# Moving columns read in two alternating halves, and activations placed two lines from the weights, in a four-layer hybrid backbone

## The chip, the cores and the metric

The kernel runs on one core of one Trainium2 chip. The metric is the device time of one execution in microseconds; of several runs the median counts.

## What is computed

The reference runs DEPTH = 2 layers over 256 latent tokens and 256 context tokens of width 1024. Each layer has a token mixer (a gated linear recurrence, RG-LRU, and a chunked gated attention, HGRN2, both in both directions, fed by one input projection) and a feed-forward part with a depthwise convolution. Nearly all arithmetic is dense products of tokens with weights:

```python
zc = hc @ lp['w_in']                 # 1024 x 9216, per layer
zl = hl @ lp['w_in']
...
p_rg = y_rg @ lp['w_proj_rg']        # 1024 x 1024
p_hg = y_hg @ lp['w_proj_hg']        # 1024 x 1024
m = jax.nn.sigmoid(z[..., O_GA:O_GA + D_MODEL]) * p_rg + jax.nn.sigmoid(z[..., O_GB:O_GB + D_MODEL]) * p_hg
return m @ lp['w_out']               # 1024 x 1024
...
u = h @ w_up                         # 1024 x 5632
return (jax.nn.silu(g) * v) @ w_down # 2816 x 1024
```

The second layer computes the outputs of the latent tokens alone, so its later products are 256 tokens wide and those of the first layer 512.

## The kernel before

Every large product is made of three TensorE products in float32r, a 4-byte format of fewer bits: an operand x is split into hi = round(x) and lo = x - hi, and hi·hi + hi·lo + lo·hi is accumulated in PSUM. Weights arrive by DMA in tiles `raw` of 1 MB; `piece` (L221) splits half a tile into `whi` (ScalarE, L233) and `wlo` (VectorE, L234). Activations lie split as well: `hi`, `lo` (the normalised input), `yh`, `yl`, `xg`, `xs`, `fh`, `fl`, `mh`, `ml`.

A matmul here has a stationary operand of 128 x 128, loaded by a weight load (LDWEIGHTS) of its own ahead of each matmul, and a moving operand of 128 x 512 or 128 x 256 columns whose product is written to as many columns of PSUM. There are two places that issue the large ones:

- `mm3` (L237, matmuls on L239 to L241) issues the three products of one k-slice of 128 rows. `feat_group` (L250) calls it for the products with features on the partitions: the weights are stationary and the activations move, 512 or 256 columns. `values` (L698) calls it with the tokens stationary and 256 columns of weights moving, and `recur` (L578) for the recurrence's gates of the first layer, with the weights `gwh`, `gwl` stationary and `xs` moving.
- `tok_product` (L490, matmuls on L500, L501, L503) is used for w_out and the down projection: the activations are stationary and 512 columns of weights move.

The trace writes a matmul as output<-stationary and moving by name, in alphabetical order, so `mm<-hi,whi` with 512 or 256 columns has `whi` stationary, and `mm<-whi,hi` is that of `values`, with `hi` stationary.

Smaller products (the attention's, the transposes, the gates of the second layer) are in plain float32, are issued elsewhere and read their columns in one run; TensorE makes two passes over a plain float32 product, and the trace has a record for each.

The order of the work is that of the Python code, with a list `side` of small steps (the modulation vectors, largely `ada_sums` on VectorE, L302) mixed in by `aside`, and a scheduler that moves instructions by priority. Where a tile lies in a partition of SBUF follows from the order of the pools and the sizes of the tiles in them. `home` (L69) takes the first piece of three pools for a filler tile; FILL gives its columns of 4 bytes. All tiles of the large products have sizes that are multiples of 256 bytes, so the fillers set where each begins within 256 bytes. With FILL = (24, 16, 24) the moving operand of every large product and the stationary operand that is loaded during it both begin 128 bytes past a multiple of 256.

Of the kernel before, what the change touches and what calls it, by code (L numbers as in the profile page):

```python
# [8 lines left out]
F32 = mybir.dt.float32  # L9
# [5 lines left out]
P = 128  # L15
# [23 lines left out]
PRI = 300  # L39
FINE = 6  # L40

FILL = (24, 16, 24)


def sub(t, off, dims):
    b = t[:]
    return bass.AP(tensor=b.tensor, offset=b.offset + off, ap=[list(b.ap[0])] + [list(d) for d in dims])


class Net:  # L50
# [18 lines left out]
    def home(self, ctx):  # L69
        for pool, n in zip((self.const, self.sm, ctx.enter_context(self.tc.tile_pool(name="pad", bufs=1, side="right"))),  # L70
                           FILL):
            if n:
# [10 lines left out]
    def psum(self):  # L83
        return self.mm.tile([P, 512], F32, tag="mm", name=self.nm("mm"))
# [5 lines left out]
    def act(self, **kw):  # L90
        ins = self.nc.scalar.activation(**kw)  # L91
        if self.last is not None:
            self.tc.add_manual_dep(ins.ins if hasattr(ins, "ins") else ins, self.last, mybir.DependencyInfo(
                mybir.DependencyClass.NoSync, mybir.DependencyReason.DATA), reason="table order")
        self.last = (ins.ins if hasattr(ins, "ins") else ins).name
        return ins
# [139 lines left out]

    def mm3(self, out, L, R, start, stop):  # L237
        nc = self.nc
        nc.tensor.matmul(out=out, lhsT=L[0], rhs=R[0], start=start, stop=False)  # L239
        nc.tensor.matmul(out=out, lhsT=L[0], rhs=R[1], start=False, stop=False)  # L240
        nc.tensor.matmul(out=out, lhsT=L[1], rhs=R[0], start=False, stop=stop)  # L241
# [64 lines left out]
    def ada_cols(self, l, m_shift, m_scale, g, store, key, ns=0):  # L306
# [22 lines left out]
        def three(i, m, j, row):  # L329
            ps = self.aux()  # L330
            nc.tensor.transpose(ps[:, 0:64 * n], row, self.ident[0:64 * n, 0:64 * n])
            close(i, m, j, sub(ps, 0, [[32, 2], [64, n]]))
# [157 lines left out]
    def tok_product(self, w, nk, act, psum):  # L490
        nc = self.nc
        pss = [[psum() for _ in range(2)] for _ in range(2)]
        pcs = {}

        def step(i, k):
            hi, lo = pcs[k]
            ah, al = act(k, i)
            for n in range(2):
                out = pss[i][n]
                nc.tensor.matmul(out=out, lhsT=ah, rhs=hi[:, n, :], start=k == 0, stop=False)  # L500
                nc.tensor.matmul(out=out, lhsT=ah, rhs=lo[:, n, :], start=False, stop=False)  # L501
            for n in range(2):
                nc.tensor.matmul(out=pss[i][n], lhsT=al, rhs=hi[:, n, :], start=False, stop=k == nk - 1)  # L503

        for k0 in range(0, nk, 2):
            raw = self.raw()
            r3 = raw.rearrange("p (k n) -> p k n", k=2)
            nc.sync.dma_start(out=r3, in_=w[k0 * P:(k0 + 2) * P, :].rearrange("(k p) n -> p k n", p=P))
            for kk in range(2):
                pcs[k0 + kk] = self.piece(r3[:, kk, :].rearrange("p (a b) -> p a b", a=2), (2, 512))  # L510
            ks = [k for k in (k0, k0 + 1) if k < nk - 3]
            for i in range(2):
                for k in ks:
                    step(i, k)
        for i in range(2):
            for k in range(nk - 3, nk):
                step(i, k)
        return pss


    def rg_phase(self, l, h, need_ctx, dr, first, more):
        nc, tc, I = self.nc, self.tc, self.ins
# [8 lines left out]
        with tc.tile_pool(name=self.nm("rg"), bufs=1, reuse_waits="tile") as pool:  # L531
# [2 lines left out]
            t2 = lambda tag, n: lambda: pool.tile([P, 2, 512], F32, tag=tag, name=self.nm(tag), bufs=n)  # L534
            R, Q, A = t2("r", 2), t2("q", 2), t2("a", 2)
            xc, g_t, gw = {}, {}, {}

            def conv(m, ps):
                t = m
                acc = XG()  # L540
                cw = lambda j: C["rcw"][:, j * 8 + t:j * 8 + t + 1]
                nc.scalar.activation(out=acc, in_=ps, func=AF.Identity, scale=cw(1), bias=C["rcb"][:, t:t + 1])
                a3, p3 = acc.rearrange("p (s t) -> p s t", s=2), ps.rearrange("p (s t) -> p s t", s=2)
                for j, (o, i) in ((0, (slice(1, S), slice(0, S - 1))), (2, (slice(0, S - 1), slice(1, S))),
                                  (3, (slice(0, S - 2), slice(2, S)))):
                    nc.vector.scalar_tensor_tensor(out=a3[:, :, o], in0=p3[:, :, i], scalar=cw(j), in1=a3[:, :, o],
                                                   op0=ALU.mult, op1=ALU.add)
                xc[t] = acc
# [13 lines left out]
            def gate_w(t):  # L562
                raw = pool.tile([P, 4, P], F32, tag="gwr", name=self.nm("gwr"), bufs=2)
                nc.gpsimd.memset(raw, 0.0)
                for u in range(2):
                    for gi, nme in enumerate(("rg_wa", "rg_wx")):
                        nc.sync.dma_start(out=raw[u * 64:(u + 1) * 64, gi::2, u * 64:(u + 1) * 64],
                                          in_=I[nme][l, :, 2 * t + u].rearrange("d i j -> i d j"))
                if exact:
                    gw[t] = (raw, raw)  # L570
                    return
                wh = pool.tile([P, 4, P], F32R, tag="gwh", name=self.nm("gwh"), bufs=2)
                wl = pool.tile([P, 4, P], F32R, tag="gwl", name=self.nm("gwl"), bufs=2)
                nc.scalar.activation(out=wh, in_=raw, func=AF.Copy)
                nc.vector.tensor_tensor(out=wl, in0=raw, in1=wh, op=ALU.subtract)
                gw[t] = (wh, wl)

            def recur(ts):  # L578
# [26 lines left out]
                for t in ts:  # L605
                    self.act(out=r[t], in_=r[t], func=AF.Sqrt, bias=self.tiny)
                    nc.vector.scalar_tensor_tensor(out=r[t], in0=a[t], scalar=1.0, in1=r[t], op0=ALU.add, op1=ALU.mult)
                    nc.vector.tensor_tensor(out=i[t], in0=i[t], in1=r[t], op=ALU.mult)
                    for d in range(2):
                        ho, at = i[t][:, d, :], a[t][:, d, :]  # L610
                        if d == 0:
                            fl = lambda x, s: x[:, s * S:(s + 1) * S]
                            last = ho[:, 2 * S - 1:2 * S]
                        else:
                            fl = lambda x, s: sub(x, (s + 1) * S - 1, [[-1, S]])
                            last = ho[:, S:S + 1]
                        nc.vector.tensor_tensor_scan(out=fl(ho, CTX), data0=fl(at, CTX), data1=fl(ho, CTX), initial=0.0,
                                                     op0=ALU.mult, op1=ALU.add)
                        nc.vector.tensor_tensor_scan(out=fl(ho, LAT), data0=fl(at, LAT), data1=fl(ho, LAT), initial=last,  # L619
                                                     op0=ALU.mult, op1=ALU.add)  # L620
                    nc.vector.tensor_tensor(out=xc[t][:, :W], in0=i[t][:, 0, :W], in1=i[t][:, 1, :W], op=ALU.add)
# [29 lines left out]
            def groups(lst, n, view):  # L651
                for _ in range(n):
# [7 lines left out]
                        continue  # L660
                    self.feat_group(w_in, c0, view, ev)

            gate_w(0), gate_w(1)
            b = 0
            for n, c in enumerate(PAT[l]):
                if c == "R":
# [572 lines left out]
```

## Time and profile before

| what | value |
|---|---|
| runs, us | 1775.95, 1782.52, 1782.79 (median 1782.52) |
| profiled execution, us | 1775.43 |
| its span, first to last instruction | 1773.6 |
| busy: TensorE matmul / weight load / VectorE / ScalarE | 96% / 81% / 72% / 52% |
| granted TensorE clock, mean | 0.994 of full speed |
| HBM read | 263.09 MB |

A matmul's busy time runs from its start to the end of its last output, and matmuls overlap, so a mean duration in the profile is longer than the distance from one start to the next. That distance is read from the timeline, which lists starts to 0.01 us. Weight loads overlap the matmul before them and have rows of their own (PEld).

### The profile page before, as it was taken

Reading aid. Unit: us, or ns where it says so; the run is one execution under the profiler, and the core shown is the slowest. Engines: PE = TensorE matmul, PEld = TensorE weight load, DVE = VectorE, ACT = ScalarE, POOL = GpSimd, SP = SyncE. Lnnn points to the kernel's source line nnn. Section 1 sums busy time; section 2 is a strip of 40 time slices with the busy share of each in tenths; the row PEclk is TensorE's granted clock in tenths of the full one; section 3 lists DMA queues with packets and bytes.
Section 4 is the critical chain, followed back from the end, with each engine's and each line's share of the span. In section 5 each row is a group of like instructions: output and inputs, shape, how many; then the busy total and the mean of one; then the engine's idle time right before and its main releaser. Section 6 shows DMA issues by size and latency. Waiting matters only on the chain.

```text
span 1773.6 us, 30755 instructions
## 1 busy us (share of the span) xinstructions
PE 1704.5 (96%) x12279; PEld 1428.8 (81%) x12279; DVE 1277.5 (72%) x2397; ACT 914.0 (52%) x1607; POOL 40.1 (2%) x65
## 2 busy tenths in 40 slices
PE   5999999999999999999999999999999999979998
PEld 3777888778878878878878877788997778979996
DVE  3787876888596897997776476777448877777754
ACT  4877723443543446433333355887444555555543
POOL 1000000000000000000000000000000000000000
PEclk9999999999999999999999999999999999989999
DMA  9422477433323277455553575333774323545563
GB/s 294 135 82 83 142 232 233 151 99 117 98 94 109 74 244 266 154 168 170 167 166 145 191 263 168 104 105 113 235 232 151 110 84 132 203 165 190 177 216 119
DMA packets 235291, 282.93 MB, mean 160 GB/s; under 512 B 18156, under 2 KB 211324, under 8 KB 235148
## 3 DMA queue, kind: packets, MB, share of 16 engines
q1 hardware_dynamic: 232156, 271.35, 46.2%
q10 hardware_dynamic: 2880, 9.51, 1.5%
q8 instruction: 96, 1.57, 0.4%
q14 instruction: 47, 0.39, 0.1%
q0 software_dynamic: 112, 0.11, 0.0%
HBM read 263.09 MB, written 17.85 MB: 158 GB/s over the span
## 4 chain that ended last, share of the span: by engine, by line
PE 81%; DVE 9%; ACT 4%; DMA 2%; issue 2%; POOL 1%; SPq 1%; POOLq 0%; DVEq 0%; ACTq 0%
PE mm L239 20%; PE mm L240 20%; PE mm L241 20%; PE mm L500 3%; PE mm L501 3%; PE mm L503 3%; DVE wlo L234 2%; PE ax L825 2%; DMA raw<-in_w_ada_dram 1%; PE ax L501 1%; PE ax L503 1%; PE ax L500 1%; DVE q L619 1%; POOL rs L405 1%; ACT r L91 1%
## 5 line engine op out<-in xcount | busy, mean ns | idle before, releaser
L240 PE MATMUL mm<-lo,whi 128*128 128x512 f32 (+1 forms) x1792 | 621.3, 347 | 6.2 <-DVE lo L440 4.6
L239 PE MATMUL mm<-hi,whi 128*128 128x512 f32 (+1 forms) x1792 | 624.6, 350 | 0.7 <-ACT whi L233 0.6
L241 PE MATMUL mm<-hi,wlo 128*128 128x512 f32 (+1 forms) x1792 | 619.0, 346 | 1.0 <-DVE wlo L234 1.0
L234 DVE TENSOR_TENSOR wlo<-raw,whi 128x1024 fp32r<-128x1024 f32 (+1 forms) x408 | 436.6, 1081 | 240.3 <-ACT whi L233 235.5
L233 ACT ACTIVATE whi<-raw 128x1024 fp32r<-128x1024 f32 (+1 forms) x408 | 378.9, 944 | 431.7 <-PE mm L240 243.0
L239 PEld LDWEIGHTS mm<-hi,whi 128*128 128x128 f32 x1792 | 340.8, 191 | 47.3 <-issue 5.1
L240 PEld LDWEIGHTS mm<-lo,whi 128*128 128x128 f32 x1792 | 340.9, 190 | 46.6 <-DVE lo L440 6.0
L241 PEld LDWEIGHTS mm<-hi,wlo 128*128 128x128 f32 x1792 | 340.9, 190 | 40.3 <-DVE wlo L234 1.6
L302 DVE SCALAR_TENSOR_TENSOR acc<-raw,s,acc 128x256 f32<-128x256 f32 x448 | 193.1, 480 | 2.1
L832 DVE TENSOR_TENSOR QK<-QK,T 128x1024 f32<-128x1024 f32 (+1 forms) x112 | 104.5, 956 | 12.4 <-PE ax L825 6.7
L841 ACT ACTIVATE kt<-QK 128x512 f32<-128x512 f32 (+1 forms) x80 | 45.1, 568 | 69.0 <-DVE QK L832 36.5
L240 PE MATMUL mm<-wlo,hi 128*128 128x256 f32 x256 | 72.7, 284 | 2.9 <-DVE wlo L234 2.9
L239 PE MATMUL mm<-whi,hi 128*128 128x256 f32 x256 | 73.3, 286 | 0.3 <-ACT whi L233 0.3
L241 PE MATMUL mm<-whi,lo 128*128 128x256 f32 x256 | 72.5, 283 | 0.0
L501 PE MATMUL mm<-wlo,fh 128*128 128x512 f32 x176 | 68.5, 389 | 0.0
L500 PE MATMUL mm<-whi,fh 128*128 128x512 f32 x176 | 68.5, 389 | 0.0
L405 POOL TENSOR_TENSOR rs<-ms,mhalf 128x1 f32<-128x1 f32 (+2 forms) x42 | 29.9, 712 | 1554.9 <-DVE ms L403 1554.9
L503 PE MATMUL mm<-whi,fl 128*128 128x512 f32 x176 | 54.2, 389 | 0.0
L240 PEld LDWEIGHTS mm<-wlo,hi 128*128 128x128 f32 x256 | 49.2, 192 | 3.6 <-DVE wlo L234 3.3
L239 PEld LDWEIGHTS mm<-whi,hi 128*128 128x128 f32 x256 | 49.1, 192 | 2.0 <-ACT xg L552 0.8
L241 PEld LDWEIGHTS mm<-whi,lo 128*128 128x128 f32 x256 | 49.2, 192 | 0.0
L91 ACT ACTIVATE acc<-acc 128x512 f32<-128x512 f32 (+1 forms) x44 | 22.6, 516 | 51.2 <-DVE acc L1046 51.2
(224 smaller groups left out, 2480.1 us busy)
## 6 DMA issues: line engine op xcount, KB each, us to landing
raw<-in_w_in_dram SPq DMA_DIRECT2D x72, 1024.0 KB
raw<-in_w_ada_dram SPq DMA_DIRECT2D x48, 1024.0 KB
raw<-in_ffn_w_up_dram SPq DMA_DIRECT2D x44, 1024.0 KB
raw<-in_ffn_w_down_dram SPq DMA_DIRECT2D x33, 1024.0 KB
raw<-in_w_out_dram SPq DMA_DIRECT2D x12, 1024.0 KB
raw<-in_w_proj_rg_dram SPq DMA_DIRECT2D x8, 1024.0 KB
raw<-in_w_proj_hg_dram SPq DMA_DIRECT2D x8, 1024.0 KB
xs<-xt SPq DMA_DIRECT2D x10, 512.0 KB
```

What stands on the lines that cost most here:

```text
L233: nc.scalar.activation(out=v(hi)[:, part, :], in_=src[:, part, :], func=AF.Copy)
L234: nc.vector.tensor_tensor(out=v(lo)[:, part, :], in0=src[:, part, :], in1=v(hi)[:, part, :], op=ALU.subtract)
L239: nc.tensor.matmul(out=out, lhsT=L[0], rhs=R[0], start=start, stop=False)
L240: nc.tensor.matmul(out=out, lhsT=L[0], rhs=R[1], start=False, stop=False)
L241: nc.tensor.matmul(out=out, lhsT=L[1], rhs=R[0], start=False, stop=stop)
L302: nc.vector.scalar_tensor_tensor(out=acc[:, st, :], in0=r3[:, k, :], scalar=s, in1=acc[:, st, :], op0=ALU.mult, op1=ALU.add)
L405: nc.gpsimd.tensor_tensor(out=rs, in0=ms, in1=self.mhalf[:, 0:n], op=ALU.pow)
L500: nc.tensor.matmul(out=out, lhsT=ah, rhs=hi[:, n, :], start=k == 0, stop=False)
L501: nc.tensor.matmul(out=out, lhsT=ah, rhs=lo[:, n, :], start=False, stop=False)
L503: nc.tensor.matmul(out=pss[i][n], lhsT=al, rhs=hi[:, n, :], start=False, stop=k == nk - 1)
L832: nc.vector.tensor_tensor(out=u, in0=u, in1=sub(t, 1, [[-1, 2], [2, W // B], [0, B]]), op=ALU.mult)
L841: nc.scalar.activation(out=kt.rearrange("p (n h j) -> p n h j", h=2, j=B), in_=sub(qk, W, [[2 * B, W // (2 * B)], [W + B, 2], [1, B]]), fu ...
```

## The change

Three things are changed. A helper `runs` rewrites the access pattern of a moving operand, and in the same way that of its output: of n columns it takes 16 from the first half, then 16 from the second half, then the next 16 of the first, and so on (16 columns of 4 bytes are 64 bytes, called a line here). `mm3` and `tok_product` use it for all their matmuls. FILL grows by 32 columns (128 bytes, two lines) in the small pool and in the right-hand pool; what lies behind these, the activations among it, moves by 128 bytes, and the weight tiles, which lie ahead of them, stay. In `rg_phase` two tiles of 32 columns are put around the gate weights, so that these lie two lines off the tiles of that pool. Then the moving and the stationary operand of nearly every large product begin 128 bytes apart within 256 (one at 0 and one at 128). Exceptions are the weights that the very first products read from the pool `ex` on the right: their tiles and the activations both begin at 0.

```diff
-FILL = (24, 16, 24)
+FILL = (24, 48, 56)
...
+def runs(ap):
+    part, (step, n) = list(ap.ap[0]), ap.ap[1]
+    assert step == 1 and n % 32 == 0
+    return bass.AP(tensor=ap.tensor, offset=ap.offset, ap=[part, [16, n // 32], [n // 2, 2], [1, 16]])
...
     def mm3(self, out, L, R, start, stop):
         nc = self.nc
+        out, R = runs(out[:, :]), [runs(r[:, :]) for r in R]
         nc.tensor.matmul(out=out, lhsT=L[0], rhs=R[0], start=start, stop=False)
...
             for n in range(2):
-                out = pss[i][n]
-                nc.tensor.matmul(out=out, lhsT=ah, rhs=hi[:, n, :], start=k == 0, stop=False)
-                nc.tensor.matmul(out=out, lhsT=ah, rhs=lo[:, n, :], start=False, stop=False)
+                out = runs(pss[i][n][:, :])
+                nc.tensor.matmul(out=out, lhsT=ah, rhs=runs(hi[:, n, :]), start=k == 0, stop=False)
+                nc.tensor.matmul(out=out, lhsT=ah, rhs=runs(lo[:, n, :]), start=False, stop=False)
             for n in range(2):
-                nc.tensor.matmul(out=pss[i][n], lhsT=al, rhs=hi[:, n, :], start=False, stop=k == nk - 1)
+                nc.tensor.matmul(out=runs(pss[i][n][:, :]), lhsT=al, rhs=runs(hi[:, n, :]), start=False, stop=k == nk - 1)
...
+            lines = lambda: pool.tile([P, 32], F32, tag=self.nm("line"), name=self.nm("line"), bufs=1)
...
+            lines()
             gate_w(0), gate_w(1)
+            lines()
```

No instruction is added, removed or put elsewhere on any engine. What differs in the instruction lists is the shape of 8088 matmuls and which instructions carry waits: 158 matmuls wait for a semaphore of TensorE itself, where 106 did. On TensorE, where `values` of the first layer goes on to its second pair of token blocks (`mm` the PSUM tiles, `whi` and `wlo` the weights that move, `hi` and `lo` the tokens), before:

```order
L240 MATMUL mm_2853<-wlo_2850,hi_89 128x256
L241 MATMUL mm_2853<-whi_2849,lo_90 128x256
L239 MATMUL mm_2903<-whi_2845,hi_89 128x256
L240 MATMUL mm_2903<-wlo_2846,hi_89 128x256
L241 MATMUL mm_2903<-whi_2845,lo_90 128x256
```

and with the change:

```order
L248 MATMUL mm_2855<-wlo_2852,hi_89 128x8x2x16
L249 MATMUL mm_2855<-whi_2851,lo_90 128x8x2x16
L247 MATMUL mm_2905<-whi_2847,hi_89 128x8x2x16 [waits PE_49]
L248 MATMUL mm_2905<-wlo_2848,hi_89 128x8x2x16
L249 MATMUL mm_2905<-whi_2847,lo_90 128x8x2x16
```

The rows are the same and stand in the same order; 256 columns have become 8 x 2 x 16, and the first matmul into a new PSUM tile waits for an earlier matmul of its own engine. In the whole program the matmul that such a wait of a large product asks for lies at least 13 matmuls ahead of the waiting one.

## Rows read from the trace of the kernel before

**Rows 1.** The page: busy time by engine, and the granted clock in 40 slices.
```profile
PE 1704.5 (96%) x12279; PEld 1428.8 (81%) x12279; DVE 1277.5 (72%) x2397; ACT 914.0 (52%) x1607; POOL 40.1 (2%) x65
...
PEclk9999999999999999999999999999999999989999
```

**Rows 2.** The page: the chain that ended last, by engine.
```profile
PE 81%; DVE 9%; ACT 4%; DMA 2%; issue 2%; POOL 1%; SPq 1%; POOLq 0%; DVEq 0%; ACTq 0%
```

**Rows 3.** Chain by line, stretches 170:676 and 60:170, in this order.
```profile
by line: PE mm L239 25.3%; PE mm L240 25.1%; PE mm L241 24.4%; PE ax L825 3.6%; PE ax L886 1.4%; DMA raw<-in_w_ada_dram 1.4%; PE ax L352 1.3%; PE mm L500 1.2%; PE mm L501 1.2%; PE mm L503 1.1%; DVE acc L302 1.1%; PE ax L923 1.0%; issue 1.0%
...
by line: PE mm L240 8.7%; PE mm L239 8.3%; PE mm L241 8.3%; DVE q L619 6.6%; ACT r L91 6.3%; DVE q L608 6.3%; DVE q L617 6.0%; issue 5.9%; DVE wlo L234 5.4%; DVE r L607 5.3%; PE ax L240 4.8%; PE ax L241 4.6%; ACT whi L233 3.8%; PE ax L239 3
```

**Rows 4.** Timeline of PE: start us, us, what; 512 columns, eleven starts apart.
```profile
542.84 0.39 PE L239 MATMUL mm<-hi,whi 128*128 128x512 f32 x1
...
545.33 0.39 PE L241 MATMUL mm<-hi,wlo 128*128 128x512 f32 x1
```

**Rows 5.** Timeline of PE, 256 columns, eighteen starts apart.
```profile
1639.77 0.28 PE L239 MATMUL mm<-hi,whi 128*128 128x256 f32 x1
...
1641.93 0.28 PE L239 MATMUL mm<-hi,whi 128*128 128x256 f32 x1
```

**Rows 6.** Timeline of PE, 256 columns, nine starts apart, at the lower clock.
```profile
722.07 0.42 PE L241 MATMUL mm<-hi,wlo 128*128 128x256 f32 x1
...
723.99 0.41 PE L241 MATMUL mm<-hi,wlo 128*128 128x256 f32 x1
```

**Rows 7.** Windows: stretch, length, busy us of PE, PEld, DVE, ACT, POOL, granted clock (PEclk).
```profile
722.20:724.60 2.40, 2.40 (x13) 2.40 (x12) 2.40 (x7) 0.82 (x2) 0.00 (x0) 0.50 0.00 0
...
543.00:545.40 2.40, 2.40 (x12) 1.90 (x11) 1.05 (x3) 0.89 (x3) 0.50 (x1) 1.00 0.00 0
```

**Rows 8.** Timeline of PE, plain float32 of 128 columns, eight starts apart.
```profile
458.86 0.39 PE L934 MATMUL ax<-v,AT 128*128 128x128 f32 x2
...
459.75 0.39 PE L934 MATMUL ax<-v,AT 128*128 128x128 f32 x2
```

**Rows 9.** Groups by line and form: count, busy us and mean ns of one.
```profile
L239 PE MATMUL mm<-hi,whi 128*128 128x512 f32 x992 | 395.7, 400 | 0.7 <-ACT whi L233 0.6 <-DVE sb L690 0.2
...
L239 PEld LDWEIGHTS mm<-hi,whi 128*128 128x128 f32 x1792 | 340.8, 191 | 47.3 <-issue 5.1 <-ACT whi L233 1.3 <-DVE sb L690 0.6
...
L825 PEld LDWEIGHTS ax<-QK,kt 128*32 128x32 f32 x1920 | 23.3, 112 | 23.5 <-issue 11.5 <-ACT kt L841 8.2 <-ACT sg L91 1.4
```

**Rows 10.** Timeline of PEld: a weight load starts with the matmul of Rows 5.
```profile
1639.77 0.19 PEld L240 LDWEIGHTS mm<-lo,whi 128*128 128x128 f32 x1
```

**Rows 11.** Windows of line L239 alone (PE, PEld): the whole span, then three stretches.
```profile
0.00:1774.00 1774.00, 795.74 (x2336) 444.21 (x2336) 0.99 0.48 159
170.00:676.00 506.00, 233.24 (x623) 117.44 (x623) 1.00 0.45 148
720.00:1030.00 310.00, 137.67 (x357) 67.89 (x357) 0.99 0.51 169
1235.00:1760.00 525.00, 270.75 (x891) 170.85 (x891) 0.99 0.52 171
```

**Rows 12.** The same windows of line L500 alone.
```profile
0.00:1774.00 1774.00, 138.03 (x360) 67.55 (x360) 0.99 0.48 159
170.00:676.00 506.00, 10.18 (x27) 5.07 (x27) 1.00 0.45 148
720.00:1030.00 310.00, 37.93 (x98) 18.40 (x98) 0.99 0.51 169
1235.00:1760.00 525.00, 43.62 (x112) 21.19 (x113) 0.99 0.52 171
```

**Rows 13.** Line L825: min/median/max ns, strided columns (QK,kt) and one run (q,sg).
```profile
L825 PE MATMUL ax<-QK,kt x1920: 190/197/263, 340.4 to 1494.7; 128*32 128x32 f32 x192
...
L825 PE MATMUL ax<-q,sg x384: 195/196/218, 339.9 to 1482.0; 128*32 128x32 f32 x192
```

**Rows 14.** Windows, columns as in Rows 7: VectorE's fullest 50 us.
```profile
700.00:750.00 50.00, 46.73 (x306) 41.73 (x306) 46.17 (x115) 26.08 (x64) 2.29 (x4) 0.97 0.44 148
```

## The prediction

> **What bounds the kernel now.** I read the page first. TensorE is busy for 96% of the span, at full clock but for a few moments [rows 1], and the chain of work that ended last lies on it for 81% [rows 2]. The chain by stretch tells where that holds: from 170 to 676 us the large products (L239 to L241, L500 to L503) have 78% of the chain, and from 60 to 170 us, where the recurrence runs beside the products, only some 38%; the rest there is VectorE and ScalarE [rows 3]. So in most of the span a nanosecond of a matmul counts, and in some stretches less than half of it does.
>
> The second view is the timeline, read for the distance from start to start, since durations overlap. With 512 columns eleven starts take 2.49 us, 226.4 ns each [rows 4]; with 256 columns eighteen take 2.16 us, 120.0 ns [rows 5]. The difference of 106.4 ns for 256 more columns is 2.4 columns per ns, one column per cycle of the full clock. At that pace 512 columns take 213.3 ns and 256 take 106.7, so each matmul has **13.1 to 13.3 ns on top**, whatever its width. Then a stretch at half clock (granted 0.50, that is 1.2 GHz [rows 7]): nine starts of 256 columns take 1.92 us, 213.3 ns each [rows 6], and 256 columns at 1.2 per ns are 213.3 ns. There nothing is on top. Plain float32 products of 128 columns start 0.89 us / 8 = 111 ns apart [rows 8], at their pace of 1.2 columns per ns 106.7, so 4.6 ns on top.
>
> A cost that is the same for both widths and goes away when the columns come at half pace belongs to something that happens once per matmul and needs the full pace to hurt. Each matmul has one weight load beside it: it starts with the matmul before [rows 5, 10]. Loads of 128 and of 32 columns last 191 and 112 ns [rows 9]; 96 columns in 79 ns are 1.2 per ns, half the pace of the moving columns. So in some 107 ns the moving operand is read over 256 columns and the stationary one over 128, and both readers begin at the same place within 256 bytes. My reading is that the faster one passes places where the slower one stands, and waits there. This is a theory: no row shows a collision, only the three distances.
>
> **The change part by part.** The new order reads 32 columns in the time of 16 weights and moves on by one line, as the weight load does, and the two begin two lines apart. If places repeat with a period of a few lines, of more than two, the readers never meet. What it is worth:
>
> - Matmuls touched: L239 has 2336 and L500 360, with L240, L241, L501 and L503 alike, so 3 x 2696 = 8088 [rows 11, 12].
> - Price of one: the 13.2 ns can go wholly (as in the rows at half clock) or down to the 4.6 ns of the plain products, which is a saving of 13.2 or of 8.6 ns. The half-clock rows are the same instructions, the plain ones run at full clock; I take the middle, **10.9 ns**.
> - On the chain: in 170:676 there are 3 x (623 + 27) = 1950, in 720:1030 3 x (357 + 98) = 1365, in 1235:1760 3 x (891 + 112) = 3009, together 6324 [rows 11, 12]. In the first of these 78.3% of 506 us are 396 us of chain, 203 ns for each of the 1950, which lies between the 120 and 226 ns of the two widths: practically every start distance is on the chain, and I take all three stretches so. 6324 x 10.9 ns = 68.9 us.
> - Elsewhere 1764 are left. There the chain's share for the large products is about 0.4 of the time [rows 3], and I count 0.4 of the saving: 7.7 us.
> - What is late next: a faster TensorE asks for split weights sooner. VectorE is busy for 46.2 us of its fullest 50 [rows 14]; the same work in 5% less time would be 97%. That still fits, but waits for `wlo` will grow. I take off 5 us, between 0 and 15.
> - The DMA queue, ScalarE and POOL get no new work. The fillers and the two tiles of the recurrence cost two memsets of 32 more columns at the start, beside the first loads: nothing, and under 0.1 us without that cover.
> - The 52 added waits of TensorE for itself ask for a matmul at least 13 places ahead, which at 120 ns a start began 1.6 us before, while a matmul lasts 0.28 to 0.40 us [rows 5, 9]: nothing. At worst each would hold for one duration, 52 x 0.4 = 21 us; since the matmul asked for has ended long before, I leave that end out.
> - Jumps: a row of 512 columns is now read and written in 32 pieces. The nearest rows are the attention's small products, with columns taken in strides or in one run: 197 and 196 ns median for 32 columns [rows 13]. So I take no cost for reading in pieces; for writing PSUM in pieces there is no row at all, and its end is under the rivals.
> - The first products that read weights from `ex` have both readers at 0. If the theory holds, these few dozen get slower instead, by 40 ns each at most (worked out below): 2 us, which I leave in the 5.
>
> Sum: 68.9 + 7.7 - 5 = 71.6 us off the profiled execution's 1775.4 us gives 1703.8. The three runs shown lie 0.5 to 7.4 us above it, median 1782.5; the runs of the change will scatter too, and I add 2 us: **1706 us**. With the ends of the price, 13.2 ns on 6324 + 706 matmuls with nothing lost gives 92.8 us (1683), and 8.6 ns with 15 us lost gives 45.5 us (1730, or 1737 with the scatter).
>
> The Trainium skill gives another floor ("TensorE: Matmul & The Clock Gate", section "Wait — 56ns, not 53.3ns?"): matmuls in a row start N / 2.4 + about 2.5 ns apart at full clock and N / 1.2 at half clock. The half-clock rows agree, and the 13 ns at full clock differ. By that floor a matmul would save 10.7 ns, and the sum would be about 1705, an estimate from that page.
>
> **The rivals.** *Half of it.* The readers keep their distance only for part of the load, because they don't start together or the pace isn't exactly half (96 columns in 79 ns is 1.22, not 1.20). For it speaks that both figures are rough; with 5 to 6 ns saved on 7030 matmuls it is some 39 us less waits: about 1742.
>
> *Nothing.* The 13 ns are a fixed price of passing from one set of weights to the next in this format, which is hidden at half clock. Nothing in the rows excludes it, since every matmul here has its own load, and all large products have the same offset, so the trace has no other offset to compare. Then the time stays at 1775 to 1783. The Trainium skill has the rule for this case ("TensorE: Matmul & The Clock Gate", section "Step-by-step: what each phase is for"): TensorE has two independent read ports into SBUF, so loading the next weights takes nothing from the running matmul. By that rule the change would do nothing; no row shows ports. I believe it less than the theory, because the price disappears with the pace.
>
> *Slower, by the jumps.* Each step from one piece of 16 to the next costs a cycle, 0.417 ns, in reading or in writing PSUM, and the saving does not come. 512 columns have 31 steps and 256 have 15; of 1792 on L239 992 are wide [rows 9], so on average some 24, or 10 ns a matmul. On 7030 matmuls that is 70 us: about 1846. It decides against the change where a step costs more than 10.9 / 24 = 0.45 ns. Against it speak the strided rows [rows 13], which are of reading alone and at half the pace. The Trainium skill's "PSUM — Partial Sum Buffer", section "Specifications (TRN2)", speaks for it: lines of PSUM have 8 bytes, and any access pattern that is not contiguous slows matmuls a good deal. Pieces of 64 bytes fill such lines, and no row here shows a matmul that writes in pieces.
>
> *Locked.* Places repeat every two lines, so the new order holds both readers at the same place for the whole load. At worst each of 128 weights holds one moving column for 0.417 ns, 53 ns in place of 13: 40 ns on 7030 matmuls, 281 us: about 2057. Against it speaks that with such a period the old order would already meet half the time, 27 ns by the same count, and 13 are seen.
>
> **How the numbers follow.** Forecast 0.68 (its own range 1683 to 1737), half of it 0.12 (1737 to 1765), nothing 0.07, jumps 0.09, locked 0.04. Faster by over 0.5%, about 9 us and what a measurement of this kernel can tell from no change, are the first two: 0.80. Same 0.07, slower 0.13. A range from 1680 to 1768 holds the first two cases and leaves out the rest, 2 in 10.
>
> **What would show it.** In the changed profile starts of 512 columns should lie 213 to 218 ns apart and of 256 columns 107 to 111, in the same stretches; TensorE's count stays, VectorE's busy time stays and its share rises to about 75%. Early, around 30 to 70 us, the products with weights from `ex` should start farther apart than their neighbours. Distances still at 226 and 120 would show the theory of meeting readers wrong, distances that grow with the width would show the jumps, and 107 and 213 with the span unchanged would show that something else had taken over the bound.

## The result, and the profile after

The change makes the kernel slower: 1821.55 us (median of 4 runs, 1819.5 to 1823.41) against 1782.26 (1775.95 to 1782.79), a ratio of the mean times of **1.0228 [1.0203, 1.0254]** (95% interval). 1706 us were forecast, with a range from 1680 to 1768, and 1821.55 lies outside it. The profiled execution has a span of 1817.6 us, 44.0 more than before.

The page's busy times and its chain by engine:

```profile
PE 1758.1 (97%) x12279; PEld 1441.6 (79%) x12279; DVE 1278.5 (70%) x2397; ACT 915.4 (50%) x1607; POOL 39.9 (2%) x65
...
PE 85%; DVE 8%; ACT 3%; DMA 1%; issue 1%; POOL 1%; SPq 1%; POOLq 0%; DVEq 0%; ACTq 0%
```

Against [rows 1, 2] TensorE has the same number of matmuls and 53.6 us more busy time; VectorE and ScalarE have what they had, within 1.4 us, and the chain's share on TensorE grows from 81 to 85%. So the time was added on TensorE, to the matmuls themselves. Which of them shows in the groups by form (busy us, mean ns of one):

```profile
L247 PE MATMUL mm<-hi,whi 128*128 128x512 f32 x992 | 407.6, 412 | 0.5 <-ACT whi L240 0.5
...
L247 PE MATMUL mm<-hi,whi 128*128 128x256 f32 x800 | 227.7, 286 | 0.0
```

The 512-wide group of the old line L239 had a mean of 400 ns [rows 9] and now has 412. The 256-wide group stands at 286, where 287 were. The timeline of TensorE gives the distances: first 512 columns, then 256, then 512 among the first 96 products, half of which have their weights from `ex`.

```profile
819.75 0.40 PE L248 MATMUL mm<-lo,whi 128*128 128x512 f32 x1
...
823.35 0.40 PE L248 MATMUL mm<-lo,whi 128*128 128x512 f32 x1
...
1683.75 0.28 PE L248 MATMUL mm<-lo,whi 128*128 128x256 f32 x1
...
1686.27 0.28 PE L248 MATMUL mm<-lo,whi 128*128 128x256 f32 x1
...
61.75 0.40 PE L249 MATMUL mm<-hi,wlo 128*128 128x512 f32 x1
...
65.35 0.40 PE L249 MATMUL mm<-hi,wlo 128*128 128x512 f32 x1
```

Fifteen starts of 512 columns take 3.60 us, **240.0 ns** each, where 226.4 were [rows 4]. Twenty-one starts of 256 columns take 2.52 us, **120.0 ns** each, as before [rows 5]. The first products stand at 240.0 ns like all others, also those with weights from `ex`, where both operands begin at 0. Over the pure time of the columns (213.3 and 106.7 ns) that is 26.7 and 13.3 ns: now in proportion to the width, 0.83 ns for each line of 16 columns that is read, two column cycles of 0.417 ns. That is a division by the width; what a single jump costs it doesn't say.

At the lower clock (the windows' last but two column is the granted clock):

```profile
520.15 0.63 PE L249 MATMUL mm<-hi,wlo 128*128 128x512 f32 x1
...
522.72 0.63 PE L249 MATMUL mm<-hi,wlo 128*128 128x512 f32 x1
...
1274.53 0.42 PE L249 MATMUL mm<-whi,lo 128*128 128x256 f32 x1
...
1276.88 0.42 PE L248 MATMUL mm<-wlo,hi 128*128 128x256 f32 x1
```
```profile
520.00:523.00 3.00, 3.00 (x8) 2.07 (x7) 1.75 (x3) 0.63 (x1) 0.00 (x0) 0.50 0.06 18
```

Six starts take 2.57 us (428 ns; 512 columns at 1.2 per ns are 427) and eleven take 2.35 us (214 ns; 213); from 1275 to 1277 us 0.50 was granted as well. As in [rows 6], nothing is on top there, also with the new order of reading.

Where in the program the 44 us come from shows in the first and last starts of the same matmuls (the view of one line; count, durations in ns, first and last start in us). Before, lines L239 and L500:

```profile
L239 PE MATMUL mm<-whi,hi x256: 278/283/678, 328.2 to 1244.6; 128*128 128x256 f32 x128
...
L239 PE MATMUL mm<-yh,whi x128: 278/386/501, 596.2 to 1543.3; 128*128 128x512 f32 x64, 128*128 128x256 f32 x64
...
L500 PE MATMUL mm<-whi,fh x176: 388/389/396, 964.1 to 1764.6; 128*128 128x512 f32 x176
```

and after, the same lines under their new numbers:

```profile
L247 PE MATMUL mm<-whi,hi x256: 279/282/683, 339.5 to 1284.3; 128*128 128x256 f32 x128
...
L247 PE MATMUL mm<-yh,whi x128: 281/394/514, 615.1 to 1582.8; 128*128 128x512 f32 x64, 128*128 128x256 f32 x64
...
L508 PE MATMUL mm<-whi,fh x176: 399/404/405, 997.7 to 1808.7; 128*128 128x512 f32 x176
```

In the order of the program the lag is 11.3, 18.9, 33.6, then 39.7, 39.5 and at the end 44.1 us. Nearly all of it is lost in the first 1245 us; from there to 1543 us nothing is, and at the end the last 512-wide products (`fh`) lose again. Of the 8088 large matmuls 4536 are 512 wide (the groups by form, added up); 4536 x 13.6 ns are 61.7 us. In the two timelines the excess over pure column time of 512-wide matmuls that start back to back grows by 52.5 us. TensorE's idle time shrinks by 9.6 us (53.6 more busy, 44.0 more span), and the span grows by 44.0.

### The profile page after: what moved, and what is told of

It is laid out like the page before. It is cut to its first block, busy times and chain, and to the rows that moved or that the text cites. A ratio compares the mean times of both kernels' runs of the same rounds, so it can differ in the third digit from the quotient of the medians.

```text
span 1817.6 us, 30775 instructions
## 1 busy us (share of the span) xinstructions
PE 1758.1 (97%) x12279; PEld 1441.6 (79%) x12279; DVE 1278.5 (70%) x2397; ACT 915.4 (50%) x1607; POOL 39.9 (2%) x65
## 4 chain that ended last, share of the span: by engine, by line
PE 85%; DVE 8%; ACT 3%; DMA 1%; issue 1%; POOL 1%; SPq 1%; POOLq 0%; DVEq 0%; ACTq 0%
PE mm L247 21%; PE mm L248 21%; PE mm L249 21%; PE mm L508 3%; PE mm L509 3%; PE mm L511 3%; DVE wlo L241 2%; PE ax L836 2%; PE ax L509 1%; PE ax L511 1%; DMA raw<-in_w_ada_dram 1%; PE ax L508 1%; PE ax L601 1%; ACT whi L240 1%; DVE q L628 1%
## 5 line engine op out<-in xcount | busy, mean ns | idle before, releaser
L248 PE MATMUL mm<-lo,whi 128*128 128x512 f32 (+1 forms) x1792 | 632.6, 353 | 4.3 <-DVE lo L448 4.3
L247 PE MATMUL mm<-hi,whi 128*128 128x512 f32 (+1 forms) x1792 | 635.2, 356 | 0.5 <-ACT whi L240 0.5
L249 PE MATMUL mm<-hi,wlo 128*128 128x512 f32 (+1 forms) x1792 | 630.3, 352 | 0.9 <-DVE wlo L241 0.9
L843 DVE TENSOR_TENSOR QK<-QK,T 128x1024 f32<-128x1024 f32 (+1 forms) x112 | 104.6, 955 | 17.3 <-PE ax L836 10.3
L1065 DVE TENSOR_TENSOR acc<-mm,acc 128x512 f32<-128x512 f32 (+1 forms) x44 | 24.4, 555 | 38.1 <-PE mm L249 36.5
```

What stands on the lines that cost most here:

```text
L843: nc.vector.tensor_tensor(out=u, in0=u, in1=sub(t, 1, [[-1, 2], [2, W // B], [0, B]]), op=ALU.mult)
```

## The experiments

**Offset and order by themselves.** A kernel without the network: rows of 48 equal matmuls into one PSUM tile, with float32r operands as in the kernel, and nothing beside them; the granted clock is 1.00 until the last rows. Each case sets the width, the order of reading and of writing, the place of the moving operand within 256 bytes against the stationary one (called offset), the stationary columns and the type.

```diff
+        for c, (dt, n, rd, wr, ph, M) in enumerate(CASES):
...
+            for i in range(REP):
+                k = i % 4
+                nc.tensor.matmul(out=sub(ps, 0, order(0, n, wr)) if M == 128 else bass.AP(
...
+                    lhsT=w[:, k * 128:k * 128 + M], rhs=sub(m, k * 512 + ph, order(0, n, rd)),
+                    start=i == 0, stop=i == REP - 1)
```

> This kernel leaves out the whole network and runs rows of 48 equal matmuls, float32r unless said, 128 stationary columns unless said, a weight load before each; the distance from start to start is read from the timeline. Theory 1 (meeting readers, plus a price per piece): in the changed kernel all distances at full clock are 26.7 ns over the pure column time with 512 columns and 13.3 with 256, which is 0.83 ns for each of 32 and 16 pieces and nothing else, so the meetings are gone. Then here: one run of columns 13 over the column time at both widths whatever the offset; pieces of 16 with an offset of 128 bytes 13 and 27, with an offset of 0 far more (up to 53); pieces of 32 with 128 bytes of offset 7 and 13; pieces of 8 at least 27 and 53; 64 or 32 stationary columns in one run 7 and 3. Theory 2 (pieces alone; the offset and the weight load do nothing): one run 13 at any number of stationary columns, because the 13 belongs to something else; pieces of 16 the same at every offset, 13 and 27; pieces of 32 and 64 never under 13. Pieces on the reading side alone or on the writing side alone tell which side pays: the one that pays has 13 and 27, the other has the 13 of one run.

The timeline of TensorE (start us, us, what); from one row's start to the next there are 48 matmuls. `taa` and `tab` are one run at offset 0, `tag` and `tah` at 192; `tai` and `taj` are pieces of 16, both in reading and in writing; `tbe` and `tbf` read in pieces only, `tbg` and `tbh` write in pieces only, at offset 128; `tbt` to `tbv` are bf16, one run of 512 columns and then pieces.

```profile
23.35 5.92 PE L101 MATMUL taa<-mr,wr 128*128 128x256 f32 x48
29.11 11.07 PE L101 MATMUL tab<-mr,wr 128*128 128x512 f32 x48
40.01 5.82 PE L101 MATMUL tac<-mr,wr 128*128 128x256 f32 x48
...
73.56 5.60 PE L101 MATMUL tag<-mr,wr 128*128 128x256 f32 x48
79.00 11.36 PE L101 MATMUL tah<-mr,wr 128*128 128x512 f32 x48
90.19 5.93 PE L101 MATMUL tai<-mr,wr 128*128 128x256 f32 x48
95.96 11.68 PE L101 MATMUL taj<-mr,wr 128*128 128x512 f32 x48
107.48 5.92 PE L101 MATMUL tak<-mr,wr 128*128 128x256 f32 x48
...
279.60 5.92 PE L101 MATMUL tbe<-mr,wr 128*128 128x256 f32 x48
285.37 11.68 PE L101 MATMUL tbf<-mr,wr 128*128 128x512 f32 x48
296.88 5.93 PE L101 MATMUL tbg<-mr,wr 128*128 128x256 f32 x48
302.65 11.36 PE L101 MATMUL tbh<-mr,wr 128*128 128x512 f32 x48
313.85 5.61 PE L101 MATMUL tbi<-mr,wr 128*64 128x256 f32 x48
...
400.34 10.52 PE L101 MATMUL tbt<-mb,wb 128*128 128x512 bf16 x48
410.70 5.40 PE L101 MATMUL tbu<-mb,wb 128*128 128x256 bf16 x48
415.94 10.52 PE L101 MATMUL tbv<-mb,wb 128*128 128x512 bf16 x48
426.30 10.88 PE L101 MATMUL tbw<-mf,wf 128*128 128x128 f32 x96
```

Worked out as (29.11 - 23.35) / 48 and so on, in ns:

| order | offset, bytes | 256 columns | 512 columns |
|---|---|---|---|
| one run | 0 | 120.0 | 227.1 |
| one run | 64 | 117.9 | 229.2 |
| one run | 128 | 118.5 | 233.3 |
| one run | 192 | 113.3 | 233.1 |
| pieces of 16, read and write | 0 to 192 | 120.0 to 120.2 | 239.8 to 240.0 |
| pieces of 8, read and write | 0 and 128 | 123.3 | 243.3 |
| pieces of 32, read and write | 0 and 128 | 119.0 and 120.0 | 236.7 |
| pieces of 64, read and write | 0 | 119.8 | 227.1 |
| read in pieces of 16 | 128 | 120.2 | 239.8 |
| write in pieces of 16 | 128 | 120.2 | 233.3 |
| one run, 32 stationary columns | 0 | 113.5 | 231.5 |
| pieces of 16, 32 stationary columns | 128 | 120.0 | 240.0 |
| bf16, one run | 0 | 109.4 | 215.8 |
| bf16, pieces of 16 | 128 | 109.2 | 215.8 |

Both distances of the network are there with nothing beside them, before (120.0 and 227.1) and after (120.0 and 240.0). Three things follow. The 13 ns for both widths are a **coincidence of offset 0**: at the other offsets 256 columns pay 7 to 12 ns and 512 pay 16 to 20. Pieces of 16 cost the same at every offset and with a quarter of the weights, so with them neither place nor length of the weight load shows. And the cost is in reading; in writing, 512 columns show none (233.3 both ways), and 256 columns 1.7 ns at this offset (120.2 against 118.5).

Neither theory of what was expected holds whole: pieces of 16 at offset 0 are no dearer than at 128, and pieces of 8 stay below the 53 and 27 ns of theory 1 (30.0 and 16.7 over column time); against theory 2, one run changes with the offset and with the stationary columns. Two more widths stood in the same kernel in one run at offset 0: 384 columns take 173.5 ns, 13.5 over column time, but 128 columns 110.6, 57 over.

**Each half of the change alone.** `e_offset` keeps the fillers and the two tiles and reads in one run; `e_runs` keeps the pieces and the old places; `e_runs32` keeps all and takes pieces of 32.

```diff
 def runs(ap):                                   e_offset
...
-    return bass.AP(tensor=ap.tensor, offset=ap.offset, ap=[part, [16, n // 32], [n // 2, 2], [1, 16]])
+    return ap
```
```diff
-FILL = (24, 48, 56)                             e_runs
+FILL = (24, 16, 24)
...
-            lines()
             gate_w(0), gate_w(1)
-            lines()
```
```diff
 def runs(ap):                                   e_runs32
...
-    return bass.AP(tensor=ap.tensor, offset=ap.offset, ap=[part, [16, n // 32], [n // 2, 2], [1, 16]])
+    return bass.AP(tensor=ap.tensor, offset=ap.offset, ap=[part, [32, n // 64], [n // 2, 2], [1, 32]])
```

> The offset of two lines alone, columns in one run. Theory 1: the faster reader passes the slower one just as often from any start, so distances stay at 226 and 120 ns and the time at 1782 (1775 to 1787). Theory 2: the same, since the offset does nothing. A third one, that the offset itself is what costs: 1800 or more, with 512 columns above 230 ns.

> The pieces of 16 alone, with the placement of the kernel before. Theory 1: both readers begin on the same line and go at the same pace, so they stay together for the whole load: distances of 256 columns well above 120 ns (up to 160) and a time well above the changed kernel's 1821, up to 2057. Theory 2: 240 and 120 ns and 1821 (1815 to 1827), as with the change.

> The change with pieces of 32 columns in place of 16. Theory 1: half as many pieces, so 13 ns over the column time with 512 columns (227 ns) and 7 with 256 (113 ns); against the changed kernel 4536 x 13.3 + 3552 x 6.7 = 84 us less, some 73 of it on the chain: about 1748. Theory 2: 13 at both widths (227 and 120 ns): about 1782, as before the change.

| kernel | median us | ratio to before | mean over column time of back-to-back starts, 512 and 256 |
|---|---|---|---|
| e_offset | 1792.7 | 1.0082 [1.006, 1.0103] | 19.2 and 12.2 ns |
| e_runs | 1824.52 | 1.0258 [1.0239, 1.0278] | 26.7 and 13.4 ns |
| e_runs32 | 1807.06 | 1.0167 [1.0142, 1.0192] | 23.4 and 13.4 ns |

The pieces alone give the whole loss; the two lines of offset, alone, also cost, since 512 columns at offset 128 go from 14 to 19 ns by the same count. Expected were at most 1787 us or at least 1800: the offset does cost, but less than the third theory had. That both together are no dearer than the pieces alone fits the row of pieces at all offsets above. Pieces of 32 missed both numbers that stood against each other: not the two readers, and not a fixed price for each step either, since half as many steps take away only 3.3 of 26.7 ns.

**Which steps cost.** The same kind of kernel again, without the network: offsets in steps of 16 bytes, the weights moved in place of the tokens, and 512 columns read line by line with a step of 2, 3, 4, 5, 8 or 16 lines.

```diff
+    if kind[0] == "j":
+        return [[16 * int(kind[1:]), n // 16], [1, 16]]
+    if kind[0] == "d":
+        return [[16, n // 32], [n // 2 + int(kind[1:]), 2], [1, 16]]
```

> Again rows of 48 equal matmuls in place of the network. What the first such run left: pieces of 16 cost 13.4 and 26.7 ns at every offset and with 32 or 128 stationary columns alike, that is 0.83 ns for each line of 16 columns, and none of it on the writing side; one run costs 7 to 13 with 256 columns and 14 to 20 with 512, depending on the offset. Theory A (same place twice in a row): the two halves lie a multiple of 256 bytes apart, so each pair of lines falls on one place of the memory; then a distance between the halves that is 128 bytes longer (two lines) costs no more than one run (7 to 14 with 256, 14 to 20 with 512), strides of 4, 8 and 16 lines cost 27 ns or more with 512 columns, and strides of 2, 3 and 5 lines clearly less. Theory B (any step away from the next line costs a beat): all distances between the halves and all strides give 13 and 27. On one run: if the offset between moving and stationary operand is what counts, weights moved by 16, 32 and 48 columns give the values of the moving operand moved by 48, 32 and 16; if the place of the moving operand by itself counts, weights moved give 13 and 14 throughout, and 32 stationary columns depend on the offset as 128 do.

The timeline, with `tbg` and `tbh` at weights moved by 64 bytes, and `tbs` to `tbw` at steps of 2, 3, 4, 5 and 8 lines:

```profile
293.19 5.62 PE L106 MATMUL tbg<-mr,wr 128*128 128x256 f32 x48
298.65 11.35 PE L106 MATMUL tbh<-mr,wr 128*128 128x512 f32 x48
...
392.97 11.68 PE L106 MATMUL tbs<-mr,wr 128*128 128x512 f32 x48
404.49 11.57 PE L106 MATMUL tbt<-mr,wr 128*128 128x512 f32 x48
415.90 11.79 PE L106 MATMUL tbu<-mr,wr 128*128 128x512 f32 x48
427.52 11.05 PE L106 MATMUL tbv<-mr,wr 128*128 128x512 f32 x48
438.41 11.78 PE L106 MATMUL tbw<-mr,wr 128*128 128x512 f32 x48
450.03 11.77 PE L106 MATMUL tbx<-mr,wr 128*128 128x512 f32 x48
```

Steps of 2, 3, 4, 8 and 16 lines start 240.0, 237.7, 242.1, 242.1 and 241.9 ns apart, but steps of **5 lines 226.9**, as one run. Neither theory foresaw that: by theory A steps of 2 and 3 would be cheap too, by theory B none would. With the weights moved by 64, 128 and 192 bytes the distances are 113.8 and 233.1, 118.8 and 233.3, 113.3 and 228.8 ns (256 and 512 columns); with the tokens moved by 192, 128 and 64 in the same kernel they are 117.9 and 233.3, 118.5 and 232.5, 113.3 and 229.0. All but one pair agree within 1 ns. So it is the distance of the two operands that counts. The odd pair is of 256 columns, and these have two levels: at 64 bytes the first kernel had 117.9 ns and this one 113.3, at 192 the other way round. The offset alone does not settle which one they take. The single starts of a row show that it settles: those of `tbg` lie 120, 117, 122 and 116 ns apart at first and 113 to 114 from the fifth on. What sets the level no run shows. With 32 stationary columns 512 columns hardly depend on the offset (230.6 to 231.7). Halves one, two or three lines farther apart change nothing for the better (239.8 to 240.2 with 512 columns).

**Reading and writing apart, in the network.** `e_write` takes only the output in pieces, `e_read` only the moving operand; both have the old places, and the cuts below are against the changed kernel. The columns of the output then come in another order, so what is computed differs from the reference; no instruction is left out.

```diff
     def mm3(self, out, L, R, start, stop):      e_write
-        out, R = runs(out[:, :]), [runs(r[:, :]) for r in R]
+        out = runs(out[:, :])
```
```diff
     def mm3(self, out, L, R, start, stop):      e_read
-        out, R = runs(out[:, :]), [runs(r[:, :]) for r in R]
+        R = [runs(r[:, :]) for r in R]
```

(and `tok_product` alike)

> The kernel before with PSUM written in pieces of 16 columns while the moving columns are read in one run, so the columns of each product land in another order and the output is not the reference's. If reading in pieces is what costs, distances stay at 226 and 120 ns and the time at 1780 (1773 to 1787). If writing PSUM in pieces is what costs, 512 columns go to 240 ns and the time to 1815 or more.

> Pieces of 16 on the reading side alone, at the placement of the kernel before; PSUM is written in one run, so the columns of each product land in another order and the output is not the reference's. If each line that is not the next one costs a beat of 0.83 ns on reading: 240 and 120 ns, and the time of pieces on both sides, 1821 to 1826. If it needs both sides: 1780.

The groups by form of 512 columns, writing:

```profile
L246 PE MATMUL mm<-hi,whi 128*128 128x512 f32 x992 | 396.3, 401 | 0.6 <-ACT whi L239 0.6
```

and reading:

```profile
L247 PE MATMUL mm<-hi,whi 128*128 128x512 f32 x992 | 407.9, 412 | 0.5 <-ACT whi L240 0.5
```

Writing in pieces: 1780.36 us, ratio 1.0008 [0.9985, 1.0032], no difference. Reading in pieces: 1821.54 us, 1.0249 [1.0227, 1.0271], all of the loss, with the means of before (400) and of after (412).

**A version from the table of offsets.** One run, as before, but the second layer's activations, which are read 256 wide in most of its products, begin 64 or 192 bytes farther. 192 is where 256 columns were cheapest in the first kernel without the network.

```diff
-        def h_tiles(key, n, side="left"):
+        def h_tiles(key, n, side="left", pad=0):
             hp = opened(key, side)
+            if pad:
+                hp.tile([P, pad], F32, tag="pad", name=self.nm("pad"))
...
-            h = h_tiles("hf", W)
+            h = h_tiles("hf", W, pad=0 if need else 48)
...
-                        h = h_tiles("h", 3 * S)
+                        h = h_tiles("h", 3 * S, pad=48)
```

(that is `e_pad192`; `e_pad64` has 16 in place of 48)

> The kernel before, columns in one run, with the second layer's activations 64 bytes farther from the weights (512-wide products of the first layer stay at offset 0). The rows of equal matmuls gave 256 columns 6.7 to 11.2 ns over the column time at 64 bytes where they had 13.2 at 0, and 512 columns 15.6 where they had 13.9. If that carries over, some 2950 matmuls of 256 columns save 2 to 6.5 ns and 420 of 512 lose 1.7: 5 to 18 us, about 1768 (1760 to 1775). If the distances in the network are set by what runs beside them and not by the offset: 1780, no change.

> The same with 192 bytes in place of 64. In rows of equal matmuls 256 columns had 6.7 to 11.1 ns and 512 columns 20. If that carries over: 2950 save 2 to 6.5 ns, 420 lose 6: 3 to 16 us, about 1771 (1763 to 1778). If the offset plays no part: 1780.

`e_pad64` takes 1768.63 us, 0.995 [0.9929, 0.9972], and **`e_pad192` 1765.78 us, 0.9938 [0.9915, 0.9961]**: faster than both kernels, by 0.6% against the one before, and both within what the offset was expected to give. The timeline of the latter, twenty-two starts of 256 columns:

```profile
1639.76 0.28 PE L241 MATMUL mm<-hi,wlo 128*128 128x256 f32 x1
...
1642.25 0.28 PE L239 MATMUL mm<-hi,whi 128*128 128x256 f32 x1
```

2.49 us / 22 are 113.2 ns. Over the back-to-back starts of the 2208 products of 256 columns that read the second layer's `hi` and `lo` the mean is 7.2 ns over column time, 10.3 in `e_pad64`, 13.2 before. 480 products of 512 columns that read the same tiles pay 20.0 and 16.4 ns, where 15.4 were. 2208 x 6.0 less 480 x 4.6 are 11.0 us; the mean times of `e_pad192` and of before lie 10.7 us apart.

**A period of four lines?** The runs so far left one rule standing: a read costs as little as one run where each line lies one line on from the last, counted modulo four lines (256 bytes). The last kernel, again without the network, tries it on steps of 6, 7, 9 and 13 lines, on lines in turn +5 and -3 (one on in both directions) or +3 and -1, and on reading backwards.

```diff
+    if kind == "m":
+        return [[-16, n // 16], [1, 16]]
+    if kind[0] == "a":
+        return [[32, n // 32], [16 * int(kind[1:]), 2], [1, 16]]
```

> Rows of 48 equal matmuls in place of the network, read in pieces of one line (16 columns), written in one run. Before this, steps of 2, 3, 4, 8 and 16 lines cost 24 to 29 ns over the column time with 512 columns, alternating halves 26.7, but steps of 5 lines 13.5, as one run does. Theory P (what counts is the step modulo four lines, and only a step of one more than a multiple of four is cheap): steps of 9 and 13 lines, and an alternation whose steps are +5 and -3 lines, cost 13 to 20 with 512 columns and 7 to 13 with 256; steps of 6 and 7, an alternation of +3 and -1, and one run backwards cost 24 to 29 with 512 and 13 to 17 with 256. Theory J (any jump costs its beat, and the one cheap value had another cause): all of these cost 24 to 29 with 512 and 13 to 17 with 256, the run backwards as one run forwards or as a jump.

The timeline, `tac` to `taf` with steps of 6, 7, 9 and 13 lines, `tai` with +5 and -3, `taj` with +3 and -1, all of 512 columns:

```profile
40.37 11.69 PE L110 MATMUL tac<-mr,wr 128*128 128x512 f32 x48
51.89 11.57 PE L110 MATMUL tad<-mr,wr 128*128 128x512 f32 x48
63.30 11.08 PE L110 MATMUL tae<-mr,wr 128*128 128x512 f32 x48
74.22 11.04 PE L110 MATMUL taf<-mr,wr 128*128 128x512 f32 x48
85.10 11.36 PE L110 MATMUL tag<-mr,wr 128*128 128x512 f32 x48
...
101.95 11.07 PE L110 MATMUL tai<-mr,wr 128*128 128x512 f32 x48
112.86 11.57 PE L110 MATMUL taj<-mr,wr 128*128 128x512 f32 x48
124.27 5.91 PE L110 MATMUL tak<-mr,wr 128*128 128x256 f32 x48
```

240.0, 237.7, **227.5, 226.7**, then **227.3** for +5/-3 and 237.7 for +3/-1: steps of one more than a multiple of four lines cost as one run, all others 10 to 15 ns more. Over both kernels steps with the same remainder modulo four agree: 241.9 to 242.1 ns for 4, 8 and 16 lines, 226.7 to 227.5 for 5, 9 and 13, 240.0 for 2 and 6, 237.7 for 3 and 7. How many of the steps are off hardly matters: a quarter of them cost 236.7 ns (pieces of 32), half of them 240.0 (pieces of 16), all of them 237.7 to 242.1. A step of 5 lines follows one run at the other offsets too (229.2, 232.5 and 233.3 ns at 64, 128 and 192). The rule also explains pieces of 64 columns, whose four lines and jump are one on each time (227.1 ns). The change's own order jumps between halves that lie a multiple of four lines apart: its steps are 0 and +1 in turn, never one run's. One miss: backwards, 512 columns stand at 233.3, between the two classes, and 256 at 117.7 ns, below their one run. The rule is shown at 512 columns alone: at 256 and offset 0 one run takes 119.8 ns, +5/-3 119.6 and +3/-1 120.0, which don't differ, and steps of 4 and 8 lines take 123.1 and 123.3.

## Why the prediction was wrong, point by point

- **The step that failed**: "Jumps: ... So I take no cost for reading in pieces". It took the price from 32-column products in plain float32 [rows 13], which run at half the pace; the new order's cost, like the old one's, is absent at that pace (428 and 214 ns at half clock, above). The rows could not show it. Measured, by `e_read` with reading alone: 0.83 ns a line, 26.7 ns for 512 columns and 13.3 for 256, so that the 10.9 ns of "Price of one", put as a saving, came as 13.6 ns lost with 512 columns and nothing with 256.
- **The rival "Slower, by the jumps"** had the right side of the matmul (reading or writing) among its two, the growth with the width as its sign, and 0.09. Its price of one cycle a step, 0.417 ns on top of the old 13, would have made 239 and 126 ns; 240.0 and 120.0 came. The new cost is two cycles a line and stands in place of the old one, so 256 columns end where they were, and the sum was 39 us more, not 70. Nor does each step have a price of its own (`e_runs32`). Its point of decision, 0.45 ns a step, was put for a saving that nothing shows: no 13 ns came back.
- **The premise** "13.1 to 13.3 ns on top, whatever its width", read as one cost per weight load, rested on one offset. At three other offsets the two widths pay differently (7 to 12 and 16 to 20 ns), and with 32 stationary columns 256 columns fall to 6.8 ns over (113.5) while 512 rise to 18. That the relative place of the weights matters was right, in one run; that two lines would be the best place was wrong, since they make 512 columns dearer (19.2 ns). Whether the two readers no longer meet in the new order, or meet behind the larger cost, no run separates.
- **"Locked"** is refuted: the products from `ex` at equal offsets and the others at two lines stand at 240.0 alike, and `e_runs`, with both operands at equal offsets throughout, takes 1824.52 us, not 2057. The 2 us taken for `ex` were wrong with it. **"Nothing"** is refuted by `e_offset`, **"Half"** by the sign.
- **The count on the chain** was somewhat high. 7030 of 8088 matmuls were counted, 0.87; of the 61.7 us that 4536 wide matmuls could lose 52.5 are seen in starts back to back, 0.85, but 44.0 reached the span, 0.71. The 5 us of other waits appear with the other sign: a slower TensorE stands idle 9.6 us less.
- **Nothing for the rest** held: VectorE's busy time (within 1.0 us), POOL's and the engines' counts on the page are those of before, the mean granted clock is 0.994 in both. The trace of after lists 20 more semaphore instructions in all, 19 of them TensorE's. The 52 added waits of TensorE for itself cost nothing, as forecast: counted in the traces, `e_write` has all 158 and the time of before, `e_read` has 106 and the whole loss.
- The Trainium skill ("TensorE: Matmul & The Clock Gate", section "Wait — 56ns, not 53.3ns?") gives N / 2.4 + about 2.5 ns. The bf16 rows agree (2.5 and 2.7 ns over); the float32r rows do not, in any order tried (6.7 to 30 ns over at 256 and 512 columns).
- The Trainium skill's rule of two independent read ports ("TensorE: Matmul & The Clock Gate", section "Step-by-step: what each phase is for") would leave the distance alone when the weights move or shrink. In one run the rows disagree: 120.0 ns with 128 stationary columns, 113.5 with 32, and 113.8 with the weights moved by 64 bytes. In pieces they agree, 120.0 with both.
- The Trainium skill ("PSUM — Partial Sum Buffer", section "Specifications (TRN2)") has every pattern that is not contiguous slow a matmul significantly. For pieces of 64 bytes `e_write` shows no such cost (1.0008).

What stays open: why a moving operand of 4 bytes loses time by the order of its lines at the upper clock, what the 256-byte period belongs to, why 256 columns take 113 or 118 ns at one and the same offset in different kernels, why 128 columns take 110.6, and why backwards lies between. That the cost is one of reading is shown in the network, and that it follows the order modulo four lines on rows of 512 float32r columns, backwards apart. bf16 was tried in one order only, in pieces of 32 bytes. A bank or a buffer behind the cost is not shown.

## What to carry to other kernels

A theory drawn from one offset and two widths should first be tried on rows of equal matmuls, with order and offset varied: one such run would have stopped this change. Keep float32r columns in one run when they move at the upper clock, or let the lines step by one more than a multiple of four (tried at 512 columns). The offset of the moving against the stationary operand is worth trying by itself: here 192 bytes for 256-wide products gave 0.6%, and for 512-wide ones 0 is the best of those measured.

## What the runs showed of the hardware that was not expected

- At offset 0, 512 float32r columns read out of line order take 237 to 243 ns (233 backwards) against 227 in order; the period is four lines of 64 bytes. For bf16 pieces of 16 columns, 32 bytes, cost nothing (215.8 ns both ways).
- Writing PSUM in pieces of 64 bytes costs nothing at 512 columns (233.3 ns both ways), nor in the network (1.0008).
- One run's cost over column time depends on the two operands' offset within 256 bytes: 6.7 to 13.3 ns with 256 columns, 13.5 to 23 with 512 (226.9 ns at 0, 236.5 at 240 bytes), and the best offset for one width is not the best for the other.
